# Layer 0's second output product in seven block products, left factors' low halves by adding DMAs, rotations in batches

## The chip, the cores and the metric

One core of a Trainium2 chip runs the whole program in one launch. The metric is device time in microseconds (us), from the first to the last instruction with what lies around it. Five engines work side by side and wait for one another by semaphores: TensorE (PE, matmuls; PEld is its weight load), VectorE (DVE), ScalarE (ACT), GpSimd (POOL) and SyncE (SP, which here only issues DMAs). POOL issues DMAs too, on the software queue.

## The reference

Two decoder layers over x of 1024 positions by 1024 channels, float32, causal, each conditioned on a vector c:

```
h, gate = ada_modulate(x, c, ...)            # RMSNorm, scale, shift; gate per channel
layer 0:  proj = h @ w_in_even               # 1024 -> 6144: xa, ga, q, k, v, gb
          ya = rg_lru(conv(xa)) * silu(ga)
          yb = stick_breaking_attention(rms(q), rms(k), v) * silu(gb)
          x  = x + gate * ([ya, yb] @ w_out_even)        # 2048 -> 1024
layer 1:  u, g = h @ w_in_odd                # 1024 -> 2048
          y = gelu(s5_ssm(u)); y = y * sigmoid(y @ glu_w + glu_b)
          x = x + gate * ((y * silu(g)) @ w_out_odd)     # 1024 -> 1024
```

## The kernel before

**Products.** Activations lie transposed: channels on the 128 partitions, 8 tiles of 1024 positions. Each float32 operand is split into a high half (a cast to float32r) and a low half (the rest), and a product is hi*hi + hi*lo + lo*hi: three matmuls of 128x128 by 128x512. `proj` (lines 112 to 130) makes one output tile of 128 channels from 8 input tiles: 8 x 6 matmuls into a pair of PSUM banks. `w_fetch` (101) loads the weight tiles of `w_order` one after the other through `raw` (two buffers), ACT casts, DVE subtracts.

**Order of the work.** PE's order is the order of the code. The order of the other engines and queues is planned by the framework, which places each instruction by readiness in its own estimate of time; at run time each engine and queue works strictly in the planned order. Pools are stacks of on-chip memory; a tile that overlays a released one waits for the last use of that one.

**Layer 0's output** (`out_even`, 1144). First eight `proj` on `ya`, then eight on `yb`, each followed by `residual`, which adds it to `x1`, 512 columns at a time. During the first eight, `yb` is loaded and split whole. After each of the second eight, `x1` of that tile is stored, squared and summed for the next norm, and scaled and split into `h1`. `rotations` (1196) makes for each of eight groups a table of 128 powers by doubling, in seven levels of widths 8 to 256 (the last in two pieces), in one buffer `rot`, and stores it for layer 1; one call stands behind each of the second eight.

**Layer 1** (`layer1`, 1222). The first three input products start on `h1` before the norm is known; `shifted` (89) makes from their raw weight tiles what the shift adds. The S5 stage keeps its tiles in pools of its own. At the end come eight `proj` with `glu_w`, then the last product.

**The last product** is already one of seven block products (Strassen's scheme in Winograd's form): 4 blocks of 256 output channels, each of 7 products, each over 4 parts of 256 input channels. `st_x` (150) makes the seven right factors of a part, high and low, `st_w` (167) the seven left factors of a block: sums `s1` to `s4` and low halves on POOL, high halves on ACT. Left factors 0 to 3 lie in the two pairs of buffers of the weight tiles (`wp`), 4 to 6 in places of their own. In block 0 the four parts are the outer loop and the products go 0, 2, 6, 4, 3, 1, 5; in blocks 1 to 3 the products go 0 to 6 with the parts inside. The right factors of part 3 can only be made when the last `glu` tile is finished.

Of the kernel before, what the change touches and what calls it, by code (L numbers as in the profile page):

```python
# [50 lines left out]
GB = 2  # L51
LRU_ORDER = "gt0 ga1 cv1 cv2 ga2 gt1 dc0 cv3 gt2 ga3 xa4 cv4 gt3 dc0 xa5 cv5 gt4 xa6 cv6 ga4 gt5 dc0 xa7 cv7 gt6 ga5 gt7 dc0 ga6 ga7"


class Trunk:
# [33 lines left out]
    def shifted(self, raw):  # L89

        v = self.nc.vector
        out = self.h1p.tile([P, P], F32, name="wsh", tag="wsh", bufs=2)
# [8 lines left out]
    def w_fetch(self, n):  # L101

        while self.w_loaded < min(len(self.w_order), n):
            hi = self.wp.tile([P, 1024], F32R, name="w_hi", tag="whi", bufs=2)
            lo = self.wp.tile([P, 1024], F32R, name="w_lo", tag="wlo", bufs=2)
            raw = self.load_split(self.w_order[self.w_loaded], hi, lo)
            if self.w_loaded in self.w_shifted:
                self.shifted(raw)
            self.w_ready.append((hi, lo))
            self.w_loaded += 1  # L110
# [39 lines left out]
    def st_x(self, hi, lo, a, b, t):  # L150
# [3 lines left out]
        b2 = b.rearrange("p (c n) -> p c n", c=2)  # L154
        v.tensor_sub(t[:, 0], a[:, h1], a[:, h0])
        act.copy(hi[:, 0], a[:, h0])
        v.tensor_sub(t[:, 2], b[:, h1], a[:, h1])
        act.copy(hi[:, 1:3], b2)
        v.tensor_sub(t[:, 1], b[:, h1], t[:, 0])
        v.tensor_sub(t[:, 3], b[:, h0], t[:, 1])  # L160
        v.tensor_sub(lo[:, 0], a[:, h0], hi[:, 0].bitcast(F32))
        v.tensor_sub(lo[:, 1:3], b2, hi[:, 1:3].bitcast(F32))
        for i in (0, 2, 1, 3):
            act.copy(hi[:, 3 + i], t[:, i])
            v.tensor_sub(lo[:, 3 + i], t[:, i], hi[:, 3 + i].bitcast(F32))

    def st_w(self, src0, src1, place, t):

        nc = self.nc
        act, pool = nc.scalar, nc.gpsimd  # L170
        a = []
        for src in (src0, src1):
            raw = self.rp.tile([P, 1024], F32, name="w_raw", tag="raw")
            nc.sync.dma_start(raw, src)
            r = raw.rearrange("p (j e m) -> p e j m", e=2, m=P)
            a += [r[:, 0], r[:, 1]]
        s1, s2, s3, s4 = t[:, 0], t[:, 1], t[:, 2], t[:, 3]
        out = []
        for i, x in enumerate((a[0], s2, a[1], s3, s1, a[3], s4)):
            if i == 1:  # L180
                pool.tensor_tensor(s1, a[2], a[3], op=ALU.add)
                pool.tensor_tensor(s2, s1, a[0], op=ALU.subtract)
            elif i == 3:
                pool.tensor_tensor(s3, a[0], a[2], op=ALU.subtract)
            elif i == 6:
                pool.tensor_tensor(s4, a[1], s2, op=ALU.subtract)
# [37 lines left out]
    def run(self):  # L224
# [12 lines left out]
        for half in range(2):  # L237
            self.w_order += [I["woe"][m][:, half * 1024:(half + 1) * 1024] for m in range(8)]
        self.s5_order = self.plan_s5()
        self.w_odd, self.w_shifted, self.wsh = len(self.w_order), set(), []  # L240
# [903 lines left out]
    def out_even(self):  # L1144
        nc, I = self.nc, self.I
        v = nc.vector
        x1p = self.pool("x1")
        x1 = self.x1 = x1p.tile([P, KT, T], F32, name="x1")
        ybp = self.pool("yb")
        ybh = ybp.tile([P, KT, T], F32R, name="yb_hi")  # L1150
        ybl = ybp.tile([P, KT, T], F32R, name="yb_lo")
        self.pair_i = 3
        ya = (self.yah, self.yal)

        def residual(m, ps):
            gate = self.mod[:, 16 + m:17 + m]
            for h in range(2):
                hs = slice(h * 512, (h + 1) * 512)
                v.scalar_tensor_tensor(x1[:, m, hs], ps[h], gate, x1[:, m, hs], op0=ALU.mult, op1=ALU.add)
# [8 lines left out]
        op = self.pool("oe")  # L1168
        acc = op.tile([P, T], F32, name="acc")
# [469 lines left out]
```

## Time and profile before

| | us |
|---|---|
| median of 3 runs | 1341.42 (1340.99 to 1341.87) |
| profiled execution, its time | 1343.34 |
| its span, first to last instruction | 1341.3 |
| PE busy | 1316.6 (98%) |
| DVE busy | 1010.6 (75%) |
| ACT busy | 651.8 (49%) |
| POOL busy | 228.9 (17%) |

The mean granted TensorE clock is 0.999 of full speed. The eight `yb` products run from 856.2 to 943.3 us, the last product from 1257.0 us to the end. The profile gives busy time by engine, the time and duration of each instruction, and for each wait what ended it. Lines (L120) are those of the kernel before. A busy share of PE counts modelled ends of matmuls; the interval between starts is the better measure of its pace.

### The profile page before, as it was taken

The numbers are of one execution on the slowest core, as the hardware profiler recorded it, in microseconds if no ns is written. First come the engines' busy times: TensorE is split into PE (matmuls) and PEld (weight loads), VectorE is DVE, ScalarE is ACT, GpSimd is POOL, SyncE is SP. The second block draws the span as 40 slices with busy tenths as digits, with TensorE's granted clock in tenths as the row PEclk, the third lists the DMA queues.
The fourth block names the chain that finished last, engine by engine and source line by source line (L and its number), as shares of the span: only waits on it lengthen the run. The fifth ranks groups of instructions, "written<-read, shape, count | busy, mean of one in ns | idle before, by whom it ended". The sixth has DMA issues, their size and how long they took to land.

```text
span 1341.3 us, 18939 instructions
## 1 busy us (share of the span) xinstructions
PE 1316.6 (98%) x7020; PEld 1137.7 (85%) x7020; DVE 1010.6 (75%) x1826; ACT 651.8 (49%) x1218; POOL 228.9 (17%) x411
## 2 busy tenths in 40 slices
PE   7998999999999999999999999999999999999998
PEld 3898989898999999988878878888888888888777
DVE  7949977777787868787999787866588669755653
ACT  6545454545454545455998621132463434632421
POOL 1012322222222222210000000000000000000784
PEclk9999999999999999999999999999999999999999
DMA  8443141414141414213112164342458778444331
GB/s 324 166 149 95 58 142 37 146 34 145 34 145 34 147 33 158 85 63 110 36 40 67 61 230 136 115 145 99 135 164 247 229 246 245 122 163 133 108 112 76
DMA packets 73356, 168.22 MB, mean 125 GB/s; under 512 B 9552, under 2 KB 35408, under 8 KB 73264
## 3 DMA queue, kind: packets, MB, share of 16 engines
q1 hardware_dynamic: 62256, 128.40, 31.3%
q0 software_dynamic: 11008, 38.62, 7.8%
q8 instruction: 55, 0.90, 0.3%
q14 instruction: 37, 0.30, 0.1%
HBM read 126.16 MB, written 40.83 MB: 125 GB/s over the span
## 4 chain that ended last, share of the span: by engine, by line
PE 78%; DVE 13%; ACT 3%; issue 3%; DMA 2%; POOL 1%; DVEq 0%; ACTq 0%; POOLq 0%
PE bank L120 6%; PE bank L121 6%; PE bank L123 6%; PE bank L122 6%; PE bank L124 6%; PE bank L125 6%; PE bank L771 6%; PE bank L773 6%; PE bank L772 6%; PE bank L837 2%; PE bank L199 2%; PE bank L197 2%; PE bank L198 2%; DMA ada_raw<-ada 2%; PE bank L849 1%
## 5 line engine op out<-in xcount | busy, mean ns | idle before, releaser
L771 PE MATMUL bank<-wqkv_hi,h_hi 128*128 128x384 f32 x512 | 173.6, 339 | 0.0
L773 PE MATMUL bank<-wqkv_hi,h_lo 128*128 128x384 f32 x512 | 172.3, 337 | 0.0
L772 PE MATMUL bank<-wqkv_lo,h_hi 128*128 128x384 f32 x512 | 172.3, 337 | 0.0
L72 ACT CAST w_hi<-w_raw 128x1024 fp32r<-128x1024 f32 x60 | 63.0, 1050 | 193.5 <-PE bank L123 148.5
L75 DVE TENSOR_TENSOR w_lo<-w_raw,w_hi 128x1024 fp32r<-128x1024 f32 x60 | 73.0, 1218 | 41.2 <-ACT w_hi L72 41.1
L771 PEld LDWEIGHTS bank<-wqkv_hi,h_hi 128*128 128x128 f32 x512 | 96.6, 189 | 0.3
L772 PEld LDWEIGHTS bank<-wqkv_lo,h_hi 128*128 128x128 f32 x512 | 96.6, 189 | 0.4
L773 PEld LDWEIGHTS bank<-wqkv_hi,h_lo 128*128 128x128 f32 x512 | 96.5, 189 | 0.0
L120 PE MATMUL bank<-h_hi,w_hi 128*128 128x512 f32 x224 | 89.1, 398 | 0.0
L122 PE MATMUL bank<-h_hi,w_hi 128*128 128x512 f32 x224 | 87.6, 391 | 0.8 <-DVE xc L1014 0.8
L124 PE MATMUL bank<-h_hi,w_lo 128*128 128x512 f32 x224 | 87.7, 392 | 0.4 <-DVE w_lo L75 0.4
L121 PE MATMUL bank<-h_lo,w_hi 128*128 128x512 f32 x224 | 87.7, 391 | 0.0
L123 PE MATMUL bank<-h_lo,w_hi 128*128 128x512 f32 x224 | 87.5, 390 | 0.0
L125 PE MATMUL bank<-h_hi,w_lo 128*128 128x512 f32 x224 | 87.4, 390 | 0.0
L778 ACT ACTIVATE nat<-bank 128x128 f32<-128x128 f32 x64 | 17.7, 277 | 141.3 <-PE bank L773 137.9
L826 DVE TENSOR_TENSOR_SCAN keep<-keep,diag 128x1024 f32<-128x1024 f32 (+3 forms) x64 | 86.2, 1347 | 0.1
L314 POOL TENSOR_SCALAR ss<-ss 128x2 f32<-128x2 f32 x64 | 28.6, 446 | 296.6 <-ACT nat L779 296.1
L820 ACT ACTIVATE keep<-bank,ss 128x512 f32<-128x512 f32 (+2 forms) x96 | 54.5, 597 | 21.7 <-PE bank L819 20.1
L783 DVE SCALAR_TENSOR_TENSOR nat<-bank,ss,gqk 128x128 f32<-128x128 f32 x64 | 22.1, 345 | 47.9 <-PE bank L837 25.9
L823 ACT ACTIVATE beta<-bank,ss 128x512 f32<-128x512 f32 (+3 forms) x96 | 54.4, 600 | 0.0
L290 DVE SCALAR_TENSOR_TENSOR ada_raw<-ada_raw,cs 128x1024 f32<-128x1024 f32 x39 | 47.6, 1220 | 7.8 <-DMA ada_raw<-ada 7.5
L315 POOL TENSOR_TENSOR ss<-ss,mh 128x2 f32<-128x2 f32 x64 | 51.9, 810 | 5.3
(436 smaller groups left out, 3739.2 us busy)
## 6 DMA issues: line engine op xcount, KB each, us to landing
ada_raw<-ada SPq DMA_DIRECT2D x39, 512.0 KB, 3.9
w_raw<-wqkv SPq DMA_DIRECT2D x21, 512.0 KB, 3.6
w_raw<-wfm SPq DMA_DIRECT2D x20, 512.0 KB, 3.6
w_raw<-woe SPq DMA_DIRECT2D x16, 512.0 KB, 3.8
w_raw<-wod SPq DMA_DIRECT2D x16, 512.0 KB, 4.4
x<-xT SPq DMA_DIRECT2D x8, 512.0 KB, 7.1
cx_s<-ce POOLq DMA_DIRECT2D x16, 256.0 KB, 2.7
win_s<-wsb POOLq DMA_DIRECT2D x16, 256.0 KB, 3.5
```

Source lines behind the costliest of these rows:

```text
L72: nc.scalar.copy(hi, raw)
L75: nc.vector.tensor_sub(lo, raw, hi.bitcast(F32))
L120: nc.tensor.matmul(ps[0], wh[:, k, :], rh[k][:, h0], start=first, stop=False)
L121: nc.tensor.matmul(ps[0], wh[:, k, :], rl[k][:, h0], start=False, stop=False)
L122: nc.tensor.matmul(ps[1], wh[:, k, :], rh[k][:, h1], start=first, stop=False)
L123: nc.tensor.matmul(ps[1], wh[:, k, :], rl[k][:, h1], start=False, stop=False)
L124: nc.tensor.matmul(ps[0], wl[:, k, :], rh[k][:, h0], start=False, stop=last)
L125: nc.tensor.matmul(ps[1], wl[:, k, :], rh[k][:, h1], start=False, stop=last)
L771: nc.tensor.matmul(ps[:, 0:384], hh[:, k, ts], wqh[:, ks], start=(k == 0), stop=False)
L772: nc.tensor.matmul(ps[:, 0:384], hh[:, k, ts], wql[:, ks], start=False, stop=False)
L773: nc.tensor.matmul(ps[:, 0:384], hl[:, k, ts], wqh[:, ks], start=False, stop=(k == KT - 1))
L826: v.tensor_tensor_scan(rev, rev, self.diag[:, T - n:T][:, ::-1], 0.0, op0=ALU.mult, op1=ALU.max)
```

## The change

- Layer 0's second output product (`yb`) takes the same seven-product form. The code of the form moves from `layer1` into `strassen`, which both layers call. Block 0 now goes 4, 5, 6, 0, 1 for parts 0 to 2, then 4, 5, 0, 1 of part 3, then 2 and 3 over all parts, and 6 of part 3 last. Blocks 1 to 3 go 4, 5, 0, 1, 2, 3, 6.
- `st_w`: the sums move to DVE. For a low half ACT writes the negated, rounded factor, and a DMA of POOL's queue adds the factor to it in place, from device memory for factors that are parts of the weights, else from the sum on chip. The weights are packed so that a half of a tile is contiguous.
- `st_x`: each factor has one tile with high and low half, and is cast and subtracted by itself.
- The right factors of parts 0 and 1 of layer 0 are made during the first six `ya` products; those of parts 2 and 3 go where `ya` was, after the last of these.
- All rotations move into the first six `ya` products: the first five levels for sixteen rows at once (`rotations_small`, twice), the two wide levels per group, two buffers `rot`. The pool of the left factors, `fw`, takes their memory.
- The places of layer 0's right factors are used again: for `h1` (made in and after the last block), for S5's tiles, for the right operand of `glu`, and for layer 1's right factors.
- `shifted` gets a load of its own after each of the first three blocks; three buffers `wsh`.

```diff
     def st_w(self, src0, src1, place, t):
...
+        v.tensor_add(s1, a[2], a[3])
+        v.tensor_sub(s2, s1, a[0])
+        v.tensor_sub(s4, a[1], s2)
+        v.tensor_sub(s3, a[0], a[2])
+        x = ((a[0], d[0]), (s2, s2), (a[1], d[1]), (s3, s3), (s1, s1), (a[3], d[3]), (s4, s4))
+        out = {}
+        for i in W_ORDER:
             hi, lo = place(i)
-            act.copy(hi, x)
-            pool.tensor_tensor(lo, x, hi.bitcast(F32), op=ALU.subtract)
-            out.append((hi, lo))
+            hf, lf = [y.rearrange("p j m -> p (j m)") for y in (hi, lo)]
+            act.copy(hf, x[i][0])
+            act.activation(lf, x[i][0], AF.Copy, scale=-1.0)
+            nc.gpsimd.dma_start(lf, x[i][1], accum_op=ALU.add)
+            out[i] = hi, lo
         return out
+
+    def strassen(self, base, ws, w_factors, x, tile, gate, scratch, after):
...
+        for u in range(4):
...
+            if u == 0:
+                order = [(i, j) for j in range(3) for i in (4, 5, 6, 0, 1)] + [(i, 3) for i in (4, 5, 0, 1)]
+                order += [(i, j) for i in (2, 3) for j in range(4)] + [(6, 3)]
+                for i, j in order:
+                    self.st_mm(b[i], ws[i], x(i, j), j, j == 0, j == 3)
...
+            else:
...
+                product(4, b[2], True, False)
+                add(xb[:, h1], b[2], gb)
+                product(5, b[3], True, True)
+                add(xb[:, h0], b[3], gb)
+                product(0, b[0], True, False)
+                nc.scalar.copy(s1, b[0])
+                product(1, b[1], True, False)
+                v.tensor_add(u2, b[1], s1)
+                product(2, b[0], False, True)
+                add(xa[:, h0], b[0], ga)
+                product(3, b[1], False, True)
+                v.tensor_add(u3, b[1], s1)
+                add(xa[:, h1], u2, ga)
+                add_u3()
+                product(6, b[2], False, True)
+                add(xa[:, h1], b[2], ga)
+            if u < 3:
+                ws = w_factors(u + 1)
+            after(u)
...
     def out_even(self):
...
-        for m in range(8):
+        self.rot_s = [self.tc.dram_tile([P, 2, 4, P], F32, name=f"rot_s{m}") for m in range(8)]
+        small = {}
+        for m in range(6):
             residual(m, self.proj(self.pair(), self.w_next(), ya))
-            self.load_split(self.yb_s[m], ybh[:, m, :], ybl[:, m, :])
+            if m in (0, 2):
+                yb_factors(m // 2)
+            if m in (0, 3):
+                small[m // 3] = self.rotations_small(m // 3, rotp)
+            for r in ((0, 1), (2,), (3,), (4, 5), (6,), (7,))[m]:
+                self.rotations(r, rotp, small[r // 4])
+        rotp.release()
+        fw = self.pool("fw")
+        residual(6, self.proj(self.pair(), self.w_next(), ya))
+        ws = w_factors(0)
+        p7 = self.proj(self.pair(), self.w_next(ahead=0), ya)
         self.yap2.release()
         self.yap.release()
...
+        yb_factors(2)
+        residual(7, p7)
+        yb_factors(3)
...
+        def h1_tile(m):
+
+            c = (3, 6, 0, 4)[m // 2]
+            hi = self.z_tile((c, 2 * (m % 2)), [P, T], F32R, "h1_hi")
+            lo = self.z_tile((c, 2 * (m % 2) + 1), [P, T], F32R, "h1_lo")
...
+        def after(u):
+            if u < 3:
+                x1_done(2 * u)
+                x1_done(2 * u + 1)
+                raw = self.rp.tile([P, 1024], F32, name="w_raw", tag="raw")
+                nc.sync.dma_start(raw, I["wod"][u])
+                self.shifted(raw)
+            else:
+                for m in range(6):
+                    h1_tile(m)
+                self.w_fetch(self.w_used + 1)
+                x1_done(7)
+                x1_done(6)
+                h1_tile(6)
+                h1_tile(7)
...
-    def rotations(self, m, pool):
+    def rotations_small(self, half, pool):
...
+        tb = pool.tile([P, 2, 16, 32], F32, name="rots", tag="rots")
...
+        for l in range(5):
             n = 1 << l
...
+            self.rotate(tb, tb[:, :, :, 0:n], slice(n, 2 * n), t1[:, :, :, 0:n], t2[:, :, :, 0:n], l, q)
...
+    def rotations(self, m, pool, small):
...
+        nc.scalar.copy(tb[:, :, :, 0:32], small[:, :, c:c + 4, :])
+        for l in (5, 6):
+            n = 1 << l
+            self.rotate(tb, tb[:, :, :, 0:n], slice(n, 2 * n), t1[:, :, :, 0:n], t2[:, :, :, 0:n], l, q)
         nc.gpsimd.dma_start(self.rot_s[m], tb)
```

`yb_factors(j)` loads two tiles of `yb` into `ybr0` and `ybr1` and calls `st_x`; `x1_done(m)` stores `x1`, squares and sums it; in `layer1`, `after` stores the output instead.

## Rows read from the trace of the kernel before

**Rows 1.** The page, busy time by engine (share of the span, instructions).
```profile
PE 1316.6 (98%) x7020; PEld 1137.7 (85%) x7020; DVE 1010.6 (75%) x1826; ACT 651.8 (49%) x1218; POOL 228.9 (17%) x411
```
**Rows 2.** Stretches: length, busy us of PE, PEld, DVE, ACT, POOL, clock, DMA share, GB/s.
```profile
778.00:856.20 78.20, 78.13 (x341) 64.15 (x342) 64.81 (x227) 14.65 (x15) 2.67 (x5) 1.00 0.47 157
856.20:943.30 87.10, 87.10 (x385) 72.07 (x384) 57.53 (x130) 23.18 (x23) 5.34 (x10) 1.00 0.32 109
```
**Rows 3.** Waits of PE from 640 us on, longest first: total us, times, longest.
```profile
PE bank L199 <- POOL w_lo L189: 2.1, 2, 1.2
```
**Rows 4.** The `yb` products: one of six groups, and PE's timeline at the end.
```profile
L120 PE MATMUL bank<-yb_hi,w_hi x64: 389/389/397, 856.2 to 942.0; 128*128 128x512 f32 x64
...
943.09 0.39 PE L125 MATMUL bank<-yb_hi,w_lo 128*128 128x512 f32 x1
```
**Rows 5.** PE's timeline, last stage: start us, us, line, operands.
```profile
1257.94 0.39 PE L198 MATMUL bank<-z_lo,w_hi 128*128 128x512 f32 x1
...
1259.52 0.40 PE L197 MATMUL bank<-z_hi,w_hi 128*128 128x512 f32 x1
...
1277.55 0.39 PE L198 MATMUL bank<-z_lo,w_hi 128*128 128x512 f32 x1
...
1279.49 0.39 PE L197 MATMUL bank<-z_hi,w_hi 128*128 128x512 f32 x1
...
1336.81 0.40 PE L199 MATMUL bank<-z_hi,w_lo 128*128 128x512 f32 x1
```
**Rows 6.** DVE's timeline in layer 0's output: residual, weight split, one rotation, `shifted`.
```profile
839.29 1.40 DVE L1159 SCALAR_TENSOR_TENSOR x<-bank,mod,x 128x512 f32<-128x512 f32 x2
840.61 1.22 DVE L75 TENSOR_TENSOR w_lo<-w_raw,w_hi 128x1024 fp32r<-128x1024 f32 x1
...
862.09 0.06 DVE L1204 MEMSET rot<- 128x4 f32 x1 [0.86 <-DMA rot_s<-rot]
...
865.63 0.43 DVE L1216 TENSOR_TENSOR rot<-rot,uw 128x256 f32<-128x256 f32 x1
...
866.95 0.43 DVE L1216 TENSOR_TENSOR rot<-rot,uw 128x256 f32<-128x256 f32 x1
...
869.28 0.28 DVE L1219 TENSOR_TENSOR rot<-rot,rot 128x128 f32<-128x128 f32 x1
...
917.58 2.68 DVE L99 SCALAR_TENSOR_TENSOR wsh<-w_raw,mod,wsh 128x128 f32<-128x128 f32 x7
```
**Rows 7.** DVE's timeline around the start of the last product.
```profile
1239.11 0.68 DVE L159 TENSOR_TENSOR st_x<-x,st_x 128x512 f32<-128x512 f32 x1
...
1256.71 4.66 DVE L165 TENSOR_TENSOR z_lo<-st_x,z_hi 128x512 fp32r<-128x512 f32 x4
...
1262.02 1.22 DVE L1487 TENSOR_TENSOR x<-sgl,gsr 128x1024 f32<-128x1024 f32 x1
...
1270.00 3.58 DVE L165 TENSOR_TENSOR z_lo<-st_x,z_hi 128x512 fp32r<-128x512 f32 x4
```
**Rows 8.** ACT's timeline, a cast of 512 columns.
```profile
1256.76 0.62 ACT L188 CAST w_hi<-w_raw 128x512 fp32r<-128x512 f32 x1 [0.77 <-PE bank L123]
```
**Rows 9.** DMA issues: tensors, queue, count, KB each, median us from issue to landing.
```profile
win_s<-wsb POOLq DMA_DIRECT2D x16, 256.0 KB, 3.5
yb_s<-yb POOLq DMA_DIRECT2D x8, 512.0 KB, 5.1
w_raw<-yb_s SPq DMA_DIRECT2D x8, 512.0 KB, 3.8
rot_s<-rot POOLq DMA_DIRECT2D x8, 512.0 KB, 2.9
us<-ut POOLq DMA_DIRECT2D x8, 512.0 KB, 7.2
```
**Rows 10.** POOL's timeline, DMAs issued one behind the other.
```profile
181.65 0.61 POOL L727 DMA_DIRECT2D win_s<-wsb  x1
...
182.95 0.54 POOL L967 DMA_DIRECT2D yb_s<-yb  x1
```

More of the change, by code (lines that the diff above doesn't have):

```diff
@@ L91, in shifted @@
         v = self.nc.vector
-        out = self.h1p.tile([P, P], F32, name="wsh", tag="wsh", bufs=2)
+        out = self.h1p.tile([P, P], F32, name="wsh", tag="wsh", bufs=3)
         self.wsh.append(out)
@@ new lines, in st_places, with place, z_tile @@
+    def st_places(self, pool):
+        two = {}
+        def place(i):
+            if i >= 4:
+                return [pool.tile([P, 4, P], F32R, name=f"w{i}_{x}", tag=f"w{i}_{x}") for x in ("hi", "lo")]
+            if i // 2 not in two:
+                two[i // 2] = [self.wp.tile([P, 2, 4, P], F32R, name=f"w_{x}", tag=f"w{x}", bufs=2) for x in ("hi", "lo")]
+            return [x[:, i % 2] for x in two[i // 2]]
+        return place
+    def z_tile(self, slot, shape, dtype, name):
+        if slot[0] is None:
+            return slot[1].tile(shape, dtype, name=name, tag=slot[2])
+        pool = self.zpool[slot[1] // 2]
+        return pool.tile(shape, dtype, name=name, tag=f"z{slot[0]}_{slot[1]}")
@@ new lines, in out_even, with yb_factors, w_factors @@
+        zs = []
+        def yb_factors(j):
+            raws = []
+            for i in range(2):
+                raws.append(fx.tile([P, T], F32, name=f"yb_raw{i}", tag=f"ybr{i}"))
+                nc.sync.dma_start(raws[i], self.yb_s[2 * j + i])
+            z = self.z_factor_tiles([(xi, j) for xi in range(7)])
+            self.st_x(z, raws[0], raws[1], fx.tile([P, 4, 512], F32, name="st_x", tag="st_x"))
+            zs.append(z)
+        def w_factors(u):
+            return self.st_w(I["woeb"][2 * u], I["woeb"][2 * u + 1], self.st_places(fw),
+                             fw.tile([P, 4, 512], F32, name="st_w", tag="st_w"))
@@ L1233, in layer1, with place @@
         us, st = {}, {}
+        names = ["win", "rot", "L", "m1", "m2", "H0", "H1", "cx", "tz", "yn", "yt", "gt"]
+        free = {n: ((1, 5, 2)[i // 4], i % 4) for i, n in enumerate(names)}
+        def place(name, shape, dtype=F32):
+            return self.z_tile(free[name], shape, dtype, name)
         def mm_pair():
@@ L1322, in s5_in @@
             v.memset(rho[:, :, 0:1], 0.0)
-            L = sp.tile([P, 2, 4, P], F32, name="L", tag="L")
+            L = place("L", [P, 2, 4, P])
             for ri in range(2):
@@ L1360, in s5_load @@
         def s5_load(m):
-            cx = sp.tile([P, 4, 2, P], F32, name="cx", tag="cx")
+            cx = place("cx", [P, 4, 2, P])
             for ri in range(2):
@@ L1374, in s5_out @@
             u = us.pop(m)
-            yn = late.tile([P, 8, P], F32, name="yn", tag="yn")
+            yn = place("yn", [P, 8, P])
             for hf in range(2):
@@ L1387, in s5_out @@
                 s5_load(m + 1)
-            yts[m] = yt = late.tile([P, T], F32, name="yt", tag="yt")
+            yts[m] = yt = place("yt", [P, T])
             nc.sync.dma_start(yt.rearrange("p (j k) -> p j k", j=8), ys.rearrange("j c g k -> (c g) j k"))
@@ L1392, in s5_gelu @@
             yt = yts.pop(m)
-            t = late.tile([P, T], F32, name="gt", tag="gt")
+            t = place("gt", [P, T])
             nc.scalar.activation(t, yt, AF.Square)
@@ L1444, in layer1 @@
         fp = self.pool("fin")
+        yh.append(y_half(7, 0))
+        yl.append(y_half(7, 1))
         self.split(y[:, 7, :], yh[7], yl[7])
-        zp = self.pool("z", side="right")
         self.pair_i = 1
         zs = []
+        h_slots = [(c, j) for c in (3, 6, 0, 4) for j in range(4)]
+        z_slots = [h_slots[0:7], h_slots[7:14], y_slots[0:7], y_slots[7:14]]
         def scratch(kind):
@@ L1553, in layer1, with tile, after @@
+            t = zs[j][self.ST_X[i]]
+            return t[:, 0], t[:, 1]
+        def tile(m):
+            nc.sync.dma_start(y[:, m, :], self.x1_s[m])
+            return y[:, m, :]
+        def after(u):
+            xa, xb = y[:, 2 * u, :], y[:, 2 * u + 1, :]
             if u < 3:
```

273 lines of the change are left out of this document (122 added, 151 removed).

## The prediction

> **What bounds the kernel now.** I read the shares of busy time first: TensorE (PE) is busy 98% of the span, VectorE (DVE) 75% [rows 1]. A share that high could still hide stages with other limits, so the table of stretches came next: from 778 to 856.2 us and from 856.2 to 943.3 us, the two halves of layer 0's output product, PE is busy for all but 0.1 us, at a granted clock of 1.00 (the 2.4 GHz level) [rows 2]. Then I read PE's waits from 640 us on: the largest is 2.1 us, two waits for `w_lo` of GpSimd (POOL) at line 189, in the very last stage [rows 3]. So a matmul less is time less, at the interval at which matmuls start there, and every new wait of PE is time more. What the change moves to DVE, ScalarE (ACT) and the DMA queues costs nothing until PE reaches it first.
>
> **Step 1, fewer matmuls in layer 0.** The second half (`yb`) has six groups of 64 = 384 matmuls, of which the first starts at 856.2 and the last at 943.09 [rows 4]: with its own interval 87.1 us, 0.2267 each. The new form has 4 blocks x 7 products x 4 parts x 3 = 336. The last stage has exactly this form already: its first block, which goes round several banks, ran from 1259.52 to 1277.55 in 79 intervals, 0.228 each; the other three, with 12 matmuls in a row into one bank, from 1279.49 to 1336.81 in 248 intervals, 0.231 each [rows 5]. So 84 x 0.228 + 252 x 0.231 = 77.4 us, and the step gives 87.1 - 77.4 = 9.7 us. Ends: 9.4 if all run at 0.231, 10.9 if all run at the old 0.2267. I take 9.7, as the form is the same.
>
> **Step 2, the last stage's two stalls.** PE lost there 1259.52 - 1257.94 - 2 x 0.228 = 1.1 us and 1279.49 - 1277.55 - 2 x 0.228 = 1.5 us, both for `w_lo` from POOL [rows 5]. The new order puts products 2 and 3 last in the first block, and the low halves no longer stand in POOL's queue. I take the whole 2.6 us; the ends are 0 (another wait in the same places) and 2.6.
>
> **Step 3, the way into layer 0's blocks.** This is where I expect to pay. The first block (start at E = 856.2) needs the left factors 4, 5, 6, 0, 1 within 2.7 us, and their places in `fw` overlay those of the rotations, so all rotations must be done. DVE is free of the stage before at about 778, where the first stretch of [rows 2] begins. One rotation took 869.28 + 0.28 - 862.09 = 7.5 us, eight of them 60 us; a level 256 wide 866.95 - 865.63 = 1.32 us [rows 6]. A level 512 wide I estimate from it at 2.15 (the multiply 0.43 at width 256, the subtract 0.29 at 128: 1.1 ns per element). The new rotation has these two levels, 3.5 us, eight times 28; the two shared beginnings are 2.4 for their narrow levels (7.5 less three times 1.32 is 3.5, of which the narrowest go) plus 1.32 and 2.15, 5.9 each. That makes 39.6 us, 20 less than before, but all of it now stands ahead of E. With seven residuals of 1.40, six `w_lo` of 1.22 [rows 6], 22 subtracts of `yb_factors` 0 and 1, four of `st_w` and four of `yb_factors(2)` at 0.68 [rows 7], DVE has 77 us to do in the 78.2 up to E (64.8 before [rows 2]). In code order the last rotation ends at about 846, ten us ahead of E. After it a factor needs two ACT passes (0.62 each [rows 8]) and one adding DMA. The trace has no such DMA. The nearest by size is a plain store of 256 KB on the same queue, 3.5 us; by bytes read and written those of 512 KB, 2.9, 5.1 and 7.2 us [rows 9]. I take 4.5, nearer to the row of its size and the middle of the others; ends 2.9 and 7.2. Factor 5 must also wait until the last rotation is stored: 846 + 2.9 [rows 9] + 1.2 + 4.5 = 854.6, against 857.3 where its low half is read. So the margin is some 2 us, with DVE full. I take 1.5 us of stall, ends 0 and 6. The upper end: factor 6 is issued behind 2 and 3, whose places come free only at E, so 6 ACT passes and a DMA, 3.7 + 4.5, against the 1.9 us after E at which it is read.
>
> **Step 4, the right factors.** `yb_factors(2)` can write once `p7` has read the places, the earliest of which come free some 7 us ahead of E; it is needed at E + 6.8 (ten triples of matmuls) and is hidden. `yb_factors(3)` gets its raw tiles only when the former is done with them: load 3.8 us [rows 9], to E + 2, then 11 subtracts 0.6 us apart plus two residual adds, to E + 10.2, and it is needed from E + 10.2 (15 triples of 0.68) to E + 10.9. I take 0.5, ends 0 and 3. In the last stage part 3 is likewise needed at 10.2 us after the start instead of 14.3, that is at 1267.2. Before, the subtracts of that part ended at 1270.00 + 3.58 = 1273.6 [rows 7]: too late by 5.7 for the new order, if nothing else changed. But these subtracts took 1.17 us (4.66 for four at 1256.71) where a like one took 0.68 at 1239.11, when POOL did nothing [rows 7]. At 0.61 apart, the nine after `y[7]` (now 1261, since the seven before are faster too) end at about 1267. I take 0.5, ends 0 and 5.7.
>
> The Trainium skill has a rule for this ("SBUF — State Buffer", "Who interferes with whom"): a DVE instruction with two SBUF inputs contends with a GpSimd instruction that reads SBUF. By it the subtracts all go back to the short time, since POOL now only issues DMAs; without it the last stage would lose those 5.7 us. The two durations above agree with it.
>
> **Step 5, later blocks.** Each next block's factors have from 8 us (factor 4 of the second block) to 14 us between the freeing of a place and its use; two ACT passes, 0.6 of issue and 4.5 make 6.3. In layer 0 the raw tiles also carry `wod` for `shifted`, which strings two loads, 2.7 us of DVE [rows 6] and an adding DMA between product 3 of one block and the block after next: about 17 us of 20. POOL's queue takes seven adding DMAs per block at 0.6, 4 us of 19.4. Each waits there for ACT's second pass; behind it stand the next adding DMAs, for which PE waits a block later, and the stores of `x1` or of the output, for which nobody waits before the end. On SP the load of `wod` waits for ACT's casts of factor 2, and the next block's raw tiles stand behind it: that is the chain of 17 us. I take 0.5 for all six block starts, ends 0 and 6.
>
> **Step 6, edges.** The `h1` tiles now come in the last block and after it. PE needs tile 0 at the end and tiles 6 and 7 only 8 us later, and ACT and DVE need 3.5 us for them; 0, ends 0 and 1.5. The way out is the same: one add, one store. Layer 1 runs the same instructions in other places; matmul intervals differ by up to 4.4 ns between forms and places (0.2267 and 0.231), and some 1150 matmuls outside the blocks change the place of their right factor. That would be 5 us if it all fell one way; I take 0 and allow a third of it, 1.7, either way.
>
> **Sum.** -9.7 - 2.6 + 1.5 + 0.5 + 0.5 + 0.5 = -9.3 us. The profiled execution took 1343.34 with a span of 1341.3; the runs' median is 1341.42, 1.9 below it. I take the difference, not the level, to the median: **1332.1 us**. Ends of the terms: all good, 1341.4 - 10.9 - 2.6 - 1.7 = 1326.2.
>
> **Rivals.**
> A. *The way in eats most of it* (steps 3 and 4 at their upper ends together). For it: DVE with 77 us of work in 78, and places that wait for one another. Against: DVE had idle pieces in the old form that waited on a single rotation buffer, and now has two. Time: -9.7 - 2.6 + 6 + 3 + 0.5 + 0.5 = -2.3, 1339.1.
> B. *Subtracts stay slow* because POOL's issuing disturbs DVE as its arithmetic did. Step 4's last-stage term becomes 5.7: 1337.3. Against: the long subtracts stand where POOL did arithmetic; no row of mine shows DVE beside a POOL that only issues.
> C. *The adding DMAs are served one after the other, and a block waits for its seven.* Place: every block start but the first, six in all. A block lasts 19.4 us. At 3.5 us each [rows 9] seven take 24.5, so PE waits 5.1 per block, 31 in all: 1332.1 + 31 = 1363, slower than before. It decides from (19.4 + 9.3/6)/7 = 3.0 us per DMA. For it: an adding transfer reads its destination too, which no row shows. Against: two plain ones on that queue, issued at 181.65 and 182.95 [rows 10], land after 3.5 and 5.1 us by the medians, 2.9 us apart for 512 KB and one more between, so plain ones overlap.
> The Trainium skill ("DMA: Bandwidth & Descriptors", "Anatomy of one DMA — SWDGE (gpsimd) path") gives about 2.0 us plus bytes over 436 GB/s, mostly completion; by this estimate one of 256 KB takes 2.6 us and seven in a row 18.2, just inside a block.
> D. *The places do not save what they should*: the 336 matmuls run, but PE waits in layer 0 for banks, since DVE in the last block has 21 us of adds, `h1` tiles and sums for 19.4. About 2 us: 1334, inside the forecast.
>
> **How the numbers follow.** Forecast (with D) 0.62, its own range 1327 to 1337; A 0.15; B 0.10; C 0.13. A difference of 0.2%, 2.7 us, is about what a measurement can tell from none. Faster (under 1338.7): 0.62 + a third of A + most of B, 0.76. Within: half of A and the rest of B, 0.10. Slower: C and the end of A, 0.14. The range runs from 1326.5 to 1342: it leaves out C and a few hundredths at either end.
>
> **What would show it.** Step 1: 336 matmuls between `p7` and the first of `h1`, with 77 to 78 us between. Step 2: no PE wait for line 189's heir. Step 3: DVE's last rotation before 848, and PE's first block without a wait on a low half; a wait of over 3 us there makes A. Step 4: DVE subtracts of 512 at 0.7 in the last stage; 1.2 makes B. Step 5: adding DMAs landing within 6 us; if they land 3 us apart and more, C. The forecast is wrong if waits of PE after 778 us sum to over 6 us, or if the blocks' matmuls start at another interval than 0.227 to 0.231.

## The result: 1.1% slower, 1356.1 us

| | before | after |
|---|---|---|
| median (runs) | 1341.35 us (4) | 1356.13 us (4) |
| lowest to highest | 1340.99 to 1341.87 | 1355.40 to 1357.16 |
| ratio | | 1.011, 95% interval 1.0093 to 1.0128 |
| profiled execution: span, mean clock | 1341.3 us, 0.999 | 1353.5 us, 0.994 |

1332.1 us was forecast, with 1326.5 to 1342 as the range: wrong, and on the wrong side. The two profiled spans differ by 12.2 us (the medians by 14.8: before's profiled run lay above its median, after's below).

The page of the changed kernel, PE's row, against [rows 1]. PE is busy for one point less of a longer span, with 48 matmuls fewer:

```profile
PE 1318.3 (97%) x6972; PEld 1131.4 (84%) x6972; DVE 1022.9 (76%) x1744; ACT 699.7 (52%) x1330; POOL 212.8 (16%) x423
```

Stretches of the changed kernel, with the columns of [rows 2]: up to the first matmul of layer 0's blocks, the blocks, layer 1 with the gate products, the last stage, and three short pieces inside them.

```profile
778.00:858.07 80.07, 78.45 (x341) 64.07 (x342) 69.76 (x160) 22.78 (x39) 8.62 (x13) 1.00 0.54 171
858.07:950.67 92.60, 82.64 (x337) 64.58 (x336) 66.86 (x104) 49.36 (x79) 23.36 (x30) 0.96 0.76 189
950.67:1266.95 316.28, 315.84 (x1691) 261.17 (x1690) 224.09 (x262) 144.32 (x202) 21.09 (x31) 1.00 0.64 187
1266.95:1349.23 82.28, 79.66 (x337) 63.88 (x335) 39.53 (x54) 30.81 (x57) 24.01 (x31) 0.98 0.70 160
869.11:873.40 4.29, 0.90 (x4) 0.19 (x2) 4.29 (x9) 3.32 (x6) 0.00 (x0) 1.00 0.00 2
873.40:877.34 3.94, 3.54 (x9) 2.33 (x10) 3.81 (x6) 2.30 (x4) 0.86 (x1) 0.57 0.11 20
1300.16:1303.90 3.74, 3.74 (x9) 2.93 (x10) 1.57 (x3) 2.03 (x4) 2.41 (x3) 0.54 0.94 219
```

And the like stretches of the kernel before:

```profile
856.23:943.32 87.09, 87.09 (x386) 72.07 (x384) 57.52 (x130) 23.16 (x23) 5.34 (x10) 1.00 0.32 109
943.32:1257.01 313.69, 312.67 (x1691) 261.27 (x1690) 220.35 (x258) 139.82 (x191) 29.71 (x34) 1.00 0.60 183
1257.01:1337.04 80.03, 77.98 (x337) 62.76 (x335) 44.93 (x48) 20.39 (x35) 54.78 (x43) 1.00 0.33 104
```

The 12.2 us lie in four places: 1.8 up to the first block (858.07 against 856.23), 5.5 in layer 0's blocks, 2.6 in layer 1 and the gate, 2.3 in the last stage. The blocks are the surprise: 336 matmuls take 5.5 us more than 384 did. PE's waits (total, times, longest) say why; in [rows 3] the largest were two for `w_lo`, 2.1 us together.

```profile
PE bank L288 <- DVE z L157: 3.5, 2, 3.1
PE bank L287 <- ACT sums L245: 3.2, 1, 3.2
PE bank L287 <- ACT st_x L245: 2.6, 1, 2.6
PE bank L289 <- DMA w_lo<-st_w: 2.2, 2, 1.7
...
PE bank L287 <- DVE sums L247: 0.8, 1, 0.8
```

A wait is not its whole price. From 869.11 PE did 0.90 us of work in 4.29; from 873.40 the granted clock is 0.57, most of it the 1.2 GHz level, and matmuls start 0.43 us apart instead of 0.23 for some 4 us. The same follows the waits of 3.2 and 2.6 us, but not the one of 1.7. So each long wait cost about 2 us more than its row says. Adding what each lengthened interval from matmul to matmul (over 0.26 us) has over the usual 0.2318, layer 0's blocks lost 14.7 us to waits and their half-clock tails, the last stage 4.7.

**Three places, three queues in order.** Around 873, ACT, SP and DVE of the changed kernel (timeline rows: start, duration, engine, line, operands, idle time before and its releaser):

```profile
857.81 0.62 ACT L191 CAST w_hi<-w_raw 128x512 fp32r<-128x512 f32 x1 [4.33 <-PE bank L122]
...
859.91 1.64 ACT L156 CAST z<-yb_raw 128x512 fp32r<-128x512 f32 x3
...
867.93 0.62 ACT L156 CAST z<-yb_raw 128x512 fp32r<-128x512 f32 x1 [4.30 <-DMA yb_raw<-yb_s]
```
```profile
861.26 1.53 SPq L1263 DMA_DIRECT2D yb_raw<-yb_s  x2
```
```profile
872.66 2.49 DVE L157 TENSOR_TENSOR z<-st_x,z 128x512 fp32r<-128x512 f32 x4
```

ACT sits idle until 857.81: the casts of block 0's factors 2 and 3, whose places come free with the last `ya` product, stand ahead of part 2's casts. Those begin at 859.91, the raw tiles of part 3 are asked for at 861.26, land 6.6 us later, and DVE ends part 3 at 875.15; PE wanted it from 870.

Around 921, block 2. SP, ACT, PE:

```profile
903.19 9.28 SPq L178 DMA_DIRECT2D w_raw<-woeb  x2
```
```profile
919.00 0.62 ACT L191 CAST w_hi<-w_raw 128x512 fp32r<-128x512 f32 x1 [6.05 <-DMA w_raw<-woeb]
...
920.56 0.57 ACT L245 COPY sums<-bank 128x512 f32<-128x512 f32 x1
```
```profile
921.19 0.55 PE L287 MATMUL bank<-z,w_hi 128*128 128x512 f32 x1 [3.16 <-ACT sums L245]
```

The copy of block 2's sums, 0.57 us long, stands behind casts for block 3 that wait for raw tiles; the bank it must free is PE's next.

Around 1300, the last stage. POOL, DVE, ACT:

```profile
1288.37 1.99 POOL L193 DMA_DIRECT2D w_lo<-st_w  x2
```
```profile
1292.03 0.75 DVE L205 SCALAR_TENSOR_TENSOR x<-bank,mod,x 128x512 f32<-128x512 f32 x1 [2.04 <-PE bank L289]
1297.76 0.69 DVE L182 TENSOR_TENSOR st_w<-w_raw 128x512 f32<-128x512 f32 x1 [4.98 <-DMA out<-x]
```
```profile
1298.48 0.62 ACT L191 CAST w_hi<-st_w 128x512 fp32r<-128x512 f32 x1 [3.71 <-DVE st_w L182]
...
1299.54 0.56 ACT L245 COPY st_x<-bank 128x512 f32<-128x512 f32 x1
```

DVE's next sums must write `st_w`, a single tile that two adding DMAs, issued at 1288.4 and 1289.1, still read. (The row names `out<-x`, the output store behind them on that queue; a store of `x` cannot hold `st_w`.) They land at 1296.2 and 1297.5, and DVE starts 0.3 us after the second. DVE waits, ACT's cast waits for DVE, the copy stands behind the cast, PE waits 2.59 us and then runs at half clock:

```profile
1300.16 0.63 PE L287 MATMUL bank<-z,w_hi 128*128 128x512 f32 x1 [2.59 <-ACT st_x L245]
```

The two landed 7.8 and 8.3 us after their issue. The 16 DMA engines had no free time in that stretch (their share, the last column but one, is 1.04 in the first row, and 1.0 is full); the like stretch of the kernel before has 0.22.

```profile
1284.00:1297.50 13.50, 13.50 (x59) 10.70 (x57) 4.12 (x5) 4.39 (x8) 4.58 (x6) 1.00 1.04 233
```
```profile
1274.06:1287.56 13.50, 12.29 (x54) 9.73 (x53) 10.82 (x13) 5.34 (x10) 11.51 (x10) 1.00 0.22 48
```

The last five transfers of POOL's queue there land 1.2 to 1.3 us apart, from 1293.7 to 1298.7. It is the same at the two other places: the share is 0.98 from 861 to 868, where part 3's raw tiles take 6.6 us, and 1.07 from 903 to 913; block 3's second raw tile, asked for at 912.1, takes 6.8. No run changes this load and nothing else, so that full DMA engines make these landings late is argued, and what it costs by itself is not shown.

My theory after this: the loss is made of such waits, each caused by the order within ACT, DVE and POOL, and not of the matmuls. The rivals: the adding DMAs are too slow or too many as such; or the waits stand behind one another, so that removing one only shows the next.

### The profile page after: what moved, and what is told of

Read it like the earlier page. It is cut to its first block, busy times and chain, and to the rows that moved or that the text cites. A ratio compares the mean times of both kernels' runs of the same rounds, so it can differ in the third digit from the quotient of the medians.

```text
span 1353.5 us, 18992 instructions
## 1 busy us (share of the span) xinstructions
PE 1318.3 (97%) x6972; PEld 1131.4 (84%) x6972; DVE 1022.9 (76%) x1744; ACT 699.7 (52%) x1330; POOL 212.8 (16%) x423
## 5 line engine op out<-in xcount | busy, mean ns | idle before, releaser
L73 ACT CAST w_hi<-w_raw 128x1024 fp32r<-128x1024 f32 x52 | 54.5, 1048 | 132.9 <-PE bank L122 100.0
L287 PE MATMUL bank<-z,w_hi 128*128 128x512 f32 x224 | 90.6, 404 | 6.9 <-ACT sums L245 3.2
L76 DVE TENSOR_TENSOR w_lo<-w_raw,w_hi 128x1024 fp32r<-128x1024 f32 x52 | 63.4, 1219 | 44.8 <-ACT w_hi L73 44.6
L288 PE MATMUL bank<-z,w_hi 128*128 128x512 f32 x224 | 90.1, 402 | 3.5 <-DVE z L157 3.5
L289 PE MATMUL bank<-z,w_lo 128*128 128x512 f32 x224 | 90.1, 402 | 2.2 <-DMA w_lo<-st_w 2.2
L287 PEld LDWEIGHTS bank<-z,w_hi 128*128 128x128 f32 x224 | 43.2, 193 | 18.7 <-ACT sums L245 3.6
```

Source lines behind the costliest of these rows:

```text
L287: mm(ps, wh[:, j], xh, start=start, stop=False, skip_group_check=True)
L288: mm(ps, wh[:, j], xl, start=False, stop=False, skip_group_check=True)
L289: mm(ps, wl[:, j], xh, start=False, stop=stop, skip_group_check=True)
```

## Experiments

All but two are single runs beside the kernel before (1341.0 to 1342.0); differences of a microsecond there mean little, so I read them by stage: time of the blocks (first to last start), what of it was lost to waits and half clock, and the same for the last stage.

| run | us | blocks, lost | last stage, lost |
|---|---|---|---|
| before | 1341.4 | 86.9, 0.0 | 79.8, 2.6 |
| after | 1356.1 | 92.4, 14.7 | 82.1, 4.7 |
| e1 sums first | 1354.64 | 94.8, 17.1 | 78.5, 1.3 |
| e2 POOL low | 1348.22 | 90.8, 13.1 | 77.3, 0.0 |
| e3 factors first | 1352.88 | 89.9, 12.2 | 82.3, 5.0 |
| e4 shift in fetch | 1351.54 | 89.2, 11.5 | 82.0, 4.6 |
| e11 = e3 + e4 | 1345.55 | 83.6, 5.9 | 82.5, 5.1 |
| e12 = e11, split scratch | 1344.50 | 87.5, 9.8 | 77.3, 0.0 |
| e13 = e11, plain halves by POOL | 1342.85 | 84.5, 6.8 | 78.1, 0.9 |
| e5 = e2 + e3 + e4 | 1340.58 | 82.4, 4.7 | 77.3, 0.0 |
| e6 = e5 + e1 | 1341.73 | 84.8, 7.1 | 77.3, 0.0 |
| e8 = e11, sums' halves by POOL | 1339.72 | 82.6, 5.0 | 77.3, 0.0 |

**The four edits alone.** From block 1 on, e1 puts the next block's factors behind this block's sums on ACT and DVE:

```diff
+                with self.tc.issue_after(act_ins.ins), self.tc.issue_after(dve_ins.ins):
+                    ws = w_factors(u + 1)
```

> The changed kernel, but from block 1 on the making of the next block's left factors stands behind this block's own sums (ACT behind the copy of product 0, DVE behind the sum with product 1). Theory S (in-order queues): PE's three waits for these sums (3.2 and 0.8 us in layer 0, 2.6 in the last stage) come from casts and sums for the next block that stand ahead of them and wait for a DMA; they go, and with them the stretches at half clock behind the two long ones (about 1.6 us each): some 10 us less, 1345 to 1349. Waits for low halves at block starts may grow by up to 2 us in all. Rival C (the adding DMAs themselves are too slow, whatever stands where): the same time comes back as waits for w_lo at the next block's start, 1354 to 1357.

The waits for sums went, in both layers. In layer 0 one of 6.0 us for `w_lo<-st_w` came instead: the factors were now themselves late.

```profile
PE bank L292 <- DMA w_lo<-st_w: 9.2, 4, 6.0
```

e2 computes the low half by a POOL subtract again:

```diff
-            act.activation(lf, x[i][0], AF.Copy, scale=-1.0)
-            nc.gpsimd.dma_start(lf, x[i][1], accum_op=ALU.add)
+            nc.gpsimd.tensor_tensor(lf, x[i][0], hf.bitcast(F32), op=ALU.subtract)
```

> The changed kernel with the low halves of the left factors by a subtract on POOL again, in both layers, in place of the negated cast and the adding DMA; the sums stay on DVE. Theory S: the sums' scratch tile is no longer held by a DMA, so the 5 us wait of DVE in the last stage and PE's 2.6 us with its half clock go (about -4.4); the waits of layer 0 at the third part's end (3.1 us) and in block 2 (3.2 us) stay, since these wait for plain loads; 1349 to 1353. DVE's subtracts beside POOL take 1.2 instead of 0.7 us. Rival C (the adding DMAs are the cause): all waits of the blocks go, 1340 to 1344.

It gained 7.9 us, about 5 of them in the last stage, which then has no stall at all. In layer 0 a 4.1 us wait for the sums' copy stayed: that one is not the adding DMAs'.

```profile
PE bank L286 <- ACT sums L244: 4.5, 2, 4.1
```

e3 makes block 0's left factors 2 and 3 (the new call in the diff) behind the right factors of part 2:

```diff
         yb_factors(2)
+        part[0]()
         residual(7, p7)
```

> The changed kernel, but in layer 0 the left factors 2 and 3 of block 0 are made behind the right factors of part 2 instead of ahead of them. Theory S: ACT no longer waits for the last ya product before it casts part 2, whose places come free up to 7 us earlier; the raw tiles of part 3 are then loaded 4 to 6 us earlier, and the waits between 869 and 877 us (0.3, 3.1 and 0.4 us and 2 us at half clock) go: about -6, 1349 to 1351. Rival P (DVE is simply full there): the wait for the low halves of part 3 stays over 2 us, 1353 to 1356.

The wait for part 3's subtracts fell from 3.1 to 0.4 us; one of 2.9 for an adding DMA of block 1 came up in its place. It gained 3.3 us.

```profile
PE bank L295 <- DVE z L157: 0.4, 1, 0.4
```
```profile
859.85 1.53 SPq L1270 DMA_DIRECT2D yb_raw<-yb_s  x2
```

The gain at part 3 is only in part ACT's order, though. One cast for factor 2 still stood ahead, so part 3's raw tiles were asked for just 1.2 us earlier, counted from the first block's start (2.0 us after it, 3.2 in the changed kernel). But the first landed 3.3 us after its issue and not 6.6: one raw tile of block 1 and the adding DMAs of factors 2 and 3 no longer stood ahead of it on the DMA engines. In all it came 4.6 us earlier.

e4 takes the raw tile for `shifted` from the regular fetch, as before the change, so that no `wod` load stands between the raw tiles of two blocks:

```diff
+            if self.w_odd <= self.w_loaded < self.w_odd + 3:
+                self.shifted(raw)
...
-                raw = self.rp.tile([P, 1024], F32, name="w_raw", tag="raw")
-                nc.sync.dma_start(raw, I["wod"][u])
-                self.shifted(raw)
```

> The changed kernel, but shifted works on the tile that w_fetch loads for the input product, as in the kernel before, so the blocks of layer 0 have no extra loads of wod between their raw tiles. Theory S: the raw tiles of blocks 2 and 3 land 4 us or more earlier, the waits at 907 (1.7) and 921 us (3.2 and 1.6 at half clock) go, 2.7 us of DVE comes back at the head of layer 1 up to three times, at most 1 us of it seen by PE: 1348 to 1352. Rival C: no change at 907 and 921, 1354 to 1357.

It gained 4.6 us, 3.2 of them in the blocks: block 2's 3.2 us wait for the sums is gone, though one of 2.1 came in block 1.

```profile
PE bank L289 <- ACT sums L247: 2.1, 1, 2.1
```

**Together.** 

> The three edits that each gained alone, together: low halves by GpSimd subtracts (-7.9 us alone), block 0's left factors 2 and 3 made behind the right factors of part 2 (-3.3), the norm's products fetched as before (-4.6). Theory S (the loss is a set of separate waits made by the order on ScalarE, VectorE and the DMA queues): the gains add up to 1340.3, so 1338 to 1342, with no matmul wait over 1.5 us in the last stage. Rival C (the waits stand behind one another, the next one shows when one is gone): 1344 to 1348, with at least one wait of 3 us or more left in layer 0's blocks.

1340.58, inside the 1338 to 1342 of the theory of separate waits. That the sum fits is in part luck: the blocks show that the waits are not simply additive. There e2, e3 and e4 alone gained 1.6, 2.5 and 3.2 us, together 10.0; e3 and e4 together (e11) 8.7. Each of these two had laid bare a wait of its own: e4's, for the sums in block 1, is gone in e11, while e3's, for block 1's adding DMA, is still there with 2.3 us. So theory and rival both hold a part.

> As the three edits together, and the next block's left factors placed behind this block's sums on ScalarE and VectorE in blocks 1 and 2. If the 4.5 us wait for ScalarE's copy of the sums in layer 0's block 2 is made by casts standing ahead of it: 2 to 5 us under the run of the three edits (1335 to 1340), no wait for sums over 1 us. Rival (the factors, made later, are then themselves late at the next block's start, as in the first run of this kind where a 6.0 us wait for w_lo came): within 1 us of the run of the three edits or up to 3 us over it.

1.2 us over e5: in the rival's range, but not by its way, for no factor came late (no wait for a `w_lo`). e5 had no wait for sums left in blocks 1 and 2, so there was nothing for the edit to gain. The blocks took 2.4 us more. About half is a longer wait for the sums in block 3, which the edit leaves alone (2.2 for 1.1 us). The rest is clock: behind the same two waits at part 3 (1.6 and 0.8 us, alike within 0.02) six matmuls of e6 ran at the 1.2 GHz level and none of e5. Those stretches, e5 and e6, with the granted clock third from the end:

```profile
868.14:873.23 5.09, 2.62 (x11) 1.53 (x9) 5.09 (x10) 2.36 (x4) 1.64 (x2) 1.00 0.00 0
```
```profile
866.76:873.82 7.06, 4.58 (x13) 3.06 (x12) 5.91 (x11) 2.93 (x5) 2.88 (x2) 0.76 0.00 0
```

So such a tail, 1.3 us here, can come or stay away behind the same waits, and single runs differ by as much in their blocks.

**Which adding DMAs hurt.** e8 keeps them for the three plain halves and gives the sums' low halves to POOL; e13 does the reverse (`is not` in the first line).

```diff
+            if x[i][0] is x[i][1]:
+                nc.gpsimd.tensor_tensor(lf, x[i][0], hf.bitcast(F32), op=ALU.subtract)
+            else:
+                act.activation(lf, x[i][0], AF.Copy, scale=-1.0)
+                nc.gpsimd.dma_start(lf, x[i][1], accum_op=ALU.add)
```

> As the three edits together, but the low halves of the factors that are a plain half of a fetched tile (0, 2, 5) again by negated cast and adding DMA from DRAM, and only the four sums' low halves by GpSimd. Theory S2 (the adding DMAs hurt because they hold the one scratch of the sums): no scratch source is left, so within 1.5 us of the run of the three edits, and the last stage without a wait over 1.5 us. Rival (an adding DMA hurts by its own landing of 5.6 us, whatever its source): 3 us or more over that run, with matmul waits on w_lo from a DMA.

As theory S2 had it: 0.9 us under e5, no stall in the last stage. Three adding DMAs per block, none from the scratch, cost nothing that a single run shows.

> Two edits on the changed kernel, block 0's left factors 2 and 3 behind the right factors of part 2 and the norm's products fetched as before; all seven low halves by negated cast and adding DMA, the four sums' from the single scratch: the base for the two runs beside it. By adding the two gains (3.3 and 4.6): 1348.2, so 1347 to 1350, with the 2.6 us wait for ScalarE's copy of the sums in the last stage's block 1 still there. If the edits overlap: 1350 to 1352.

Better than the sum of the two gains. Beside e5, which differs only in the low halves, the seven adding DMAs cost 5.2 us in the last stage (82.5 against 77.3); the 1.3 more in the blocks is no more than one half-clock tail.

e12 gives each of the four sums a tile of its own in both layers (the diff shows layer 0's), with no more memory and all seven adding DMAs:

```diff
-        s1, s2, s3, s4 = [t[:, i] for i in range(4)]
+        s1, s2, s3, s4 = t
...
-                             fw.tile([P, 4, 512], F32, name="st_w", tag="st_w"), part)
+                             [fw.tile([P, 512], F32, name=f"st_w{i}", tag=f"st_w{i}") for i in range(4)], part)
```

> The base of two edits, and the scratch of a left factor's four sums in four tiles of their own in place of one (no more memory), so that each comes free with its own adding DMA. If the whole tile's hold, up to the last of its four DMAs, makes the late sums: the wait in the last stage's block 1 goes and layer 0's block 2 gains, 3 to 8 us under the base (1340 to 1345). Rival (the DMAs' own landing, 5 to 7 us from a scratch tile, is what is late, and each sum's first use is bound by the DMA that reads it whatever the tile): within 2 us of the base.

The total, 1.1 us under the base, would be the rival's. By stage it is two things. The last stage lost its stall whole; DVE's first sum there, in e11 and in e12 (whose last stages begin at 1256.40 and 1260.74):

```profile
1287.57 0.69 DVE L184 TENSOR_TENSOR st_w<-w_raw 128x512 f32<-128x512 f32 x1 [5.35 <-DMA out<-x]
```
```profile
1287.36 0.69 DVE L184 TENSOR_TENSOR st_w<-w_raw 128x512 f32<-128x512 f32 x1 [3.59 <-DMA w_raw<-woo]
```

31.2 us into the stage in e11, 26.6 in e12, which now waits for its raw tile only. The four DMAs that read the sums landed as late in both, the last 30.9 and 30.5 us into the stage: with seven adding DMAs the whole tile's hold made that stall. And in layer 0 the same DMA, issued 18.9 us after the blocks' start in both runs, landed later; PE, e11 and e12:

```profile
880.34 0.50 PE L298 MATMUL bank<-z,w_lo 128*128 128x512 f32 x1 [2.26 <-DMA w_lo<-st_w]
```
```profile
882.91 0.80 PE L298 MATMUL bank<-z,w_lo 128*128 128x512 f32 x1 [4.21 <-DMA w_lo<-st_w]
```

That is block 1's factor 4, issued at 874.98 and 875.62: 5.4 and 7.3 us to its use. In both runs this DMA and the 512 KB load issued 1.2 us behind it were through some 4.5 us after the landing before them; in e11 the DMA was done first, in e12 both ended together. Why, I can't say. The blocks took 3.9 us more, 2.7 of them here.

> The counterpart of the run with mixed low halves (1339.7): here the four sums' low halves come by adding DMA from the scratch, and the three plain halves' (0, 2, 5) by a GpSimd subtract. If the source in the scratch is what hurts: within 3 us of the base of two edits (1346 to 1350), with the same waits. If the number of adding DMAs hurts (four per set here, three there, seven in the base): 1340 to 1343.

1342.85 is where I had put the theory of the number, and against "the source in the scratch hurts by itself": four from the scratch, with three subtracts on POOL beside them, cost the last stage 0.9 us, not 5, and landed after 4.7 us by the median (5.5 in e11). The tile is free when the last of its four has landed, and that is 28.6 us into the stage here and 30.9 in e11; DVE's first sum starts 0.2 and 0.3 us behind it. That the hold makes the stall is shown by e12, and that it is shorter with four by these landings; that they come earlier because the DMA engines carry less (a share of 0.82 from 1278 to 1287, 1.06 from 1276 to 1287.3 in e11) is argued.

**Places.** e7 is the changed kernel with h1's high and low halves in other ones of the same sixteen places.

```diff
-            c = (3, 6, 0, 4)[m // 2]
-            hi = self.z_tile((c, 2 * (m % 2)), [P, T], F32R, "h1_hi")
-            lo = self.z_tile((c, 2 * (m % 2) + 1), [P, T], F32R, "h1_lo")
+            ch, cl = ((3, 6), (0, 4))[m // 4]
+            hi = self.z_tile((ch, m % 4), [P, T], F32R, "h1_hi")
+            lo = self.z_tile((cl, m % 4), [P, T], F32R, "h1_lo")
```

> The changed kernel with layer 1's input h1 in the same sixteen places, but the high and low half of a tile in other ones of them (factors 3 and 6, and 0 and 4, of one part, in place of two parts of one factor). Theory of places (the time from matmul to matmul hangs on where the two halves stand): the mean interval in layer 1's input products moves from 231.1 ns by at least 1 ns, 768 matmuls, so the time by 0.8 us or more (1352.5 to 1355.3 if shorter); gate products (230.6 ns), whose places are unchanged, stay. Rival (the interval is set by something else, as the clock or the weights' places): 231.1 +- 0.3 ns and 1355.4 to 1357.2.

1354.69. Over runs of 96 matmuls the mean interval fell from 232.0 to 231.5 ns, and by the measure of the expectation from 231.1 to 230.4: more than the rival's 0.3, less than the 1 that I had named. The time from the blocks' end to the last stage fell by 0.5 us. Single tiles moved more: the pair at factors 3 and 6 of part 3 has 228.9, that of part 0 231.3; gate products stayed at 230.6.

**A version that beats both.** e9 is e8 with e7's places and, in block 3, the casts of h1 tiles 3 to 5 behind the sums; e10 is e9 with high and low half exchanged in h1 and in the gate's operand.

```diff
+                with self.tc.issue_after(self.sum_ins[0].ins), self.tc.issue_after(self.sum_ins[1].ins):
+                    for m in range(3, 6):
+                        h1_tile(m)
```

> The run with mixed low halves (1339.7), with two more edits: the places of h1's halves as in the run on places (1.4 us less there), and in layer 0's block 3 the casts of h1 tiles 3 to 5 behind the sums (the matmul wait of 2.2 us at 930.8 there: ScalarE copied the sums only at 930.17, behind three h1 casts of 3.22 us). If both do alone what the traces say: 1336 to 1338.5, no wait for the sums in block 3. Rival (the casts, put later, are late for layer 1's first products, and the way into layer 1 grows by what block 3 lost): 1338 to 1340.

> The same as the run before it, but high and low half change places with each other in h1 (all eight tiles) and in the gate products' operand (tiles 0 to 6). If the interval goes by the distance of the two halves alone, it stays: 230.0 ns in layer 1's input products and 230.5 in the gate's, within 0.3 each, and the time within 1 us of that run. If it goes by which place each half has, the intervals of single tiles change by 1 to 4 ns, and their mean by 0.5 or more in at least one of the two.

Ten runs each against 19 of before (median 1341.39): e9 1339.91, ratio 0.9987 (0.9977 to 0.9996), in the rival's band, though not by its way: the stretch up to the last stage is no longer than e8's, but a wait of 1.6 us for DVE's sums is left in block 3; e10 1339.03, ratio 0.998 (0.9971 to 0.9989). Both beat the kernel before, by 0.1 and 0.2%, e10 by 2.4 us; the exchange left the mean intervals as they were (231.5 ns over runs of 96, 230.6 in the gate), and those of single tiles. e10's blocks and last stage, columns as above, and its largest waits in the blocks:

```profile
856.89:939.13 82.24, 78.97 (x337) 62.82 (x336) 68.80 (x91) 42.53 (x65) 29.43 (x29) 1.00 0.53 144
...
1255.07:1332.56 77.49, 77.49 (x337) 62.90 (x335) 43.47 (x55) 24.71 (x45) 30.04 (x31) 1.00 0.48 126
```
```profile
PE bank L301 <- DVE z L159: 2.0, 2, 1.2
PE bank L300 <- DVE sums L259: 0.6, 1, 0.6
PE bank L300 <- ACT sums L257: 0.6, 1, 0.6
```

## Why the prediction was wrong

- **Step 1** (-9.7): right in kind. Without what was lost to waits the blocks take 77.7 us in after and 77.6 in e5, against 86.9: -9.2, short of the near end (-9.4 was said, but 336 x 0.231 makes it 9.5). One matmul takes 0.2318, not 0.228 to 0.231.
- **Step 2** (-2.6): right. The two POOL stalls are gone, and a last stage without stalls takes 77.3 us against 79.8 (e2, e5, e8, e12).
- **Step 3** (+1.5): the size about right, 2.6 us, though in part by luck. The last rotation ended at 845.7, 846 was said. But the first block began 1.8 us later for another cause than the one feared, 1.24 of it a wait for DVE's `w_lo` of a `ya` product at 814.92. Inside the block 0.8 us went at factor 6's low half, which I had named; its DMA was issued ahead of factors 2 and 3, at 853.85, and landed 6.8 us later, where 4.5 was taken. Rival A's way in is out.
- **Step 4** (+0.5 and +0.5): the last-stage half is right; DVE's subtracts of 512 are back at 0.68, so rival B is out. The trace agrees with the rule of the Trainium skill that the prediction cites ("SBUF — State Buffer", "Who interferes with whom"): 1.17 beside POOL's arithmetic before, 0.68 where POOL only issues DMAs, and 1.15 to 1.28 for DVE's sums `s2` and `s4` in e2, where POOL subtracts again. `yb_factors(3)` was mis-sized: with its half clock it cost 5.9 us where 0.5, at most 3, was said. I had part 2's casts start when their places were free, and did not ask what stood ahead of them on ACT: four passes for block 0's factors 2 and 3, released only with the last `ya` product; nor what stood ahead of part 3's raw tiles on the DMA engines (3.8 us was taken to their landing, 6.6 measured). e3 shows that the order of the two made it.
- **Step 5** (+0.5, at most 6): this is the step that failed. Layer 0's later blocks lost 8 us and the last stage's second 4.4 to waits and half clock, 12.4 in all. I asked whether the next block's factors are in time for their use; mostly they are. What is late is this block's own copy of the sums, 0.57 us long, behind those factors' casts on ACT. The `wod` chain was named, but as a danger to the factors; e4 shows its price, and that PE pays it at the copy. And nowhere did I ask who waits for the *source* of an adding DMA: the scratch of the sums, which POOL used to read in order.
- **Step 6** (0 ± 1.7): too narrow. 96 matmuls of layer 1's input in a row and the gate's 384, before and after, by their first and last starts:

```profile
1147.87 0.48 PE L120 MATMUL bank<-h_hi,w_hi 128*128 128x512 f32 x1
...
1169.71 0.39 PE L125 MATMUL bank<-h_hi,w_lo 128*128 128x512 f32 x1
1169.94 0.39 PE L120 MATMUL bank<-y_hi,w_hi 128*128 128x512 f32 x1
...
1256.78 0.39 PE L125 MATMUL bank<-y_hi,w_lo 128*128 128x512 f32 x1
```
```profile
1156.15 0.48 PE L119 MATMUL bank<-h_hi,w_hi 128*128 128x512 f32 x1
...
1178.19 0.39 PE L124 MATMUL bank<-h_hi,w_lo 128*128 128x512 f32 x1
1178.42 0.40 PE L119 MATMUL bank<-y_hi,w_hi 128*128 128x512 f32 x1
...
1266.73 0.39 PE L124 MATMUL bank<-y_hi,w_lo 128*128 128x512 f32 x1
```

That is 229.9 to 232.0 ns and 226.7 to 230.6. If all input products moved like these 96, 768 x 2.1 + 384 x 3.8 = 3.1 us; the whole stretch, with all else in it, grew by 2.6. It nearly all fell one way.

- **Rival C** had the right sign, but no block waited for seven transfers in a row. Where the DMA engines were full, transfers did land one after the other, but 1.2 to 1.3 us apart, not the 3.0 that it needed. The adding DMAs cost 0.86 us of POOL each (0.6 was taken) and landed late (4.5 was taken):

```profile
w_lo<-st_w POOLq DMA_DIRECT2D x32, 256.0 KB, 6.0
```

The Trainium skill ("DMA: Bandwidth & Descriptors", "Anatomy of one DMA — SWDGE (gpsimd) path") gives about 2.0 us plus bytes over 436 GB/s for one DMA, an estimate of 2.6 here. The measurement decides: 6.0, and 3.2 to 10.7 over all of them in the blocks.

- **Half clock** was in no term. Of the 19.4 us lost in both output products, 12.6 are waits of PE; the other 7 are matmuls after the three long ones and the steps back into the stream. The prediction's own sign showed too: PE's waits after 778 us sum to 14.8, where over 6 were to make it wrong.

By terms: -9.2 (step 1) - 2.5 (step 2) + 1.8 (the way in) + 14.7 and 4.7 (lost in the two products) + 2.6 (step 6) = +12.1 us, of the 12.2 measured between the spans.

## What to carry to other kernels

When work moves to an engine with idle time, list what stands behind it in that engine's queue, not only who needs its result: a copy of half a microsecond that frees TensorE's bank was worth 5 us here. A transfer that replaces an engine's read also takes over the hold on the source, until the whole tile's last transfer has landed; tiles of their own for each piece give it back. And read the share of the DMA engines where such transfers are added: where it was 1.0 here, loads came late too (6.6 and 6.8 us, where `yb`'s took 3.8 before). Where matmuls run without gaps, price a wait of some 3 us at 5, and a new place of an operand at a few nanoseconds per matmul.

## What was not expected of the hardware

The interval from matmul to matmul (512 columns, full clock) depends on where the moving operand's two halves stand: 226.7 ns for gate tiles before, single tiles from 226.7 to 231.7 after; e7 shows it for `h1` by an edit of the places alone, and exchanging the halves changes nothing (e10). Which distance is good is open. Adding DMAs of 256 KB landed 3.2 to 10.7 us after their issue; one and the same of them, issued 18.9 us after the blocks' start, took 5.4 us to its use in e11 and 7.3 in e12, two kernels that differ in the tiles of the sums alone. And half clock came behind a pair of waits in e6 and not behind the same pair in e5.
